# One convolution block's taps moved to TensorE, and attention values with the values stationary, in a two-layer encoder kernel

## The chip, the core and the metric

The kernel runs on one core of a Trainium2 chip. The metric is the device time of one execution in microseconds (us). A core has a matrix engine (TensorE, PE in the profile; PEld is its loading of the stationary operand), VectorE (DVE), ScalarE (ACT), GpSimd (POOL), and SyncE (SP), whose queue issues most DMAs. Each engine runs its own instructions in a fixed order. One that waits for another engine holds up everything behind it on its own engine.

## The reference

```python
for l in range(DEPTH):                       # DEPTH = 2
    x = x + 0.5 * swiglu(rms_norm(x, ffn1_norm[l]), ...)
    h = rms_norm(x, mix_norm[l]);  p = h @ w_in[l]
    attn = mla_group(...)                    # 8 heads, q and k of 96, v of 64, softmax over allowed keys
    conv = conv_group(p[..., o_cv:], ...)    # below
    x = x + jnp.concatenate([attn, conv], axis=-1) @ w_out[l]
    x = x + 0.5 * swiglu(rms_norm(x, ffn2_norm[l]), ...)
    x = rms_norm(x, post_norm[l])
...
u = a * sigmoid(g)                           # 512 channels
y = causal depthwise convolution of u, 31 taps per channel, + conv_b
conv = silu(layer_norm(y, ln_g, ln_b))
...
probs = softmax(masked scores);  out = einsum('bhqk,bhkd->bqhd', probs, v)
```

x is 512 tokens by 1024 features, float32.

## The kernel before

Activations lie with features in the 128 partitions and the 512 tokens along the row. Every large product is done as three matmuls of rounded halves (`mm3`, lines 144 to 146: hi by hi, hi by lo, lo by hi). Such a group of 24 matmuls gives 128 output features (8 blocks of 128 inputs, 3 matmuls each). `load_w` loads a weight tile over SP's queue into one of three `raw` buffers and splits it (ACT makes hi, DVE makes lo; for the output weights of kind "sum" POOL issues a DMA that adds, line 137).

A layer is FFN 1, the mixing block (`mix_body`) and FFN 2. The steps ahead of attention in the mixing block are listed in `SEQ`: c1, c2 and c3 are the input projections of the convolution's channel blocks (c0 is done ahead of the list). Each takes two groups of 24 matmuls, and then a gate (`glu`) that leaves the block's input u[c]. `uk` makes keys and values (`keys`): after its matmuls, ACT, DVE and POOL normalise the keys into `kn`, token block by token block, the last step of each being a power on POOL and products on DVE (lines 664 to 670).

Attention goes head by head in stages with lags (`ORDER`): `turn` transposes q and k of a head; `scores` makes four blocks of scores (128, 256, 384 and 512 keys wide), their maxima on DVE and the exponentials on ACT; `turn_p` transposes the exponentials in ten 128 by 128 blocks and copies them out of PSUM; `values` multiplies them with v, and for each pair of heads divides by the sums; `turn_out` transposes the pair's result, so that features are in the partitions again.

The 31 taps of the four channel blocks are applied in the ways that `CONV` names:

- "D" (c0 and c3): ACT writes the first tap and the bias into a PSUM bank (the tag "cv" has one buffer), then DVE adds 30 taps there, one instruction each (line 791), and ACT copies the bank out (line 801).
- "A" (c1 and c2): ACT makes 30 products (line 795, tag "pr", three buffers), POOL adds each of them to y (line 799). The adds of c1 from the 16th tap on and all of c2 are set to be issued after the keys' last power on POOL.

The sum of the four y (POOL, lines 813 to 815) goes into a matmul (line 817) that gives the mean for the LayerNorm. On PE the output projection's first groups (`early_groups`) stand behind that matmul. The order of instructions on each engine comes from a scheduler with its own estimate of times; it is fixed when the program is built.

Of the kernel before, what the change touches and what calls it, by code (L numbers as in the profile page):

```python
# [7 lines left out]
FP = mybir.dt.float32  # L8
# [17 lines left out]
DV = 64  # L26
# [3 lines left out]
CK = 31  # L30
# [3 lines left out]
WC = 1024  # L34
# [34 lines left out]

@with_exitstack  # L70
def encoder_kernel(ctx: ExitStack, tc: tile.TileContext, xT, consts, vecs, rgain, wgu1, wd1,
                   wcv, wql, wkl, wuq, wkv, wout, wgu2, wd2, out):
    nc = tc.nc
    PSUM = bass.MemoryType.PSUM
    cpool = ctx.enter_context(tc.tile_pool(name="const", bufs=1))
# [24 lines left out]
    V, A, G, T = nc.vector, nc.scalar, nc.gpsimd, nc.tensor  # L100
# [9 lines left out]
    ident = cst[:, CID:CID + P]  # L110
# [37 lines left out]
    def split(src, w=S):  # L148
        hi, lo = slot(FR, w), slot(FR, w)
        A.copy(hi, src)  # L150
        V.tensor_tensor(lo, src, hi.bitcast(FP), ALU.subtract)
        return hi, lo
# [350 lines left out]

    def mix_body(kpool, l, gx, norm, done):
        u, order = [], {}
        ys = [None if kind == "D" else kpool.tile([P, S], FP, tag="y", name=nm("y"), bufs=2) for kind in CONV]

        def glu(pa, pg):
            tg = tmp()
# [20 lines left out]
        cqT, ckT, pq, scqs, vs = [], [], [], [], []  # L530
# [143 lines left out]
        rm = norm()  # L674
        for step in SEQ.split():
            if step == "R":
                R = norm()
# [8 lines left out]
        at = []  # L686
# [3 lines left out]
        heads = [{} for _ in range(H)]  # L690
# [14 lines left out]
        def scores(h):  # L705
            qT, kT = heads[h]["qk"]
            b01, b2, b3 = bank(), bank(), bank()
            if h % 2 == 0:
                heads[h]["sums"] = small.tile([P, NT, 2], FP, tag="sums", name=nm("sums"), bufs=3)
            sums = heads[h - h % 2]["sums"]  # L710
            mx = small.tile([P, NT], FP, tag="mx", name=nm("mx"), bufs=3)
            pi = []
            ps = [slot() for _ in range(3)]
            ps = [ps[0][:, 0:128], ps[0][:, 128:384], ps[1][:, 0:384], ps[2]]
            for i in range(NT):
                n = (i + 1) * P
                o = (b01[:, 0:128], b01[:, 128:384], b2[:, 0:384], b3)[i]
                T.matmul(o, qT[0:DQ, i * P:(i + 1) * P], kT[0:DQ, 0:n], start=True, stop=False)  # L718
                heads[h]["s"] = T.matmul(o[:, n - 64:n], mrow, mneg, start=False, stop=True).ins
                V.tensor_reduce(mx[:, i:i + 1], o, axis=AX.X, op=ALU.max, negate=True)  # L720
# [24 lines left out]
        def values(h):  # L745

            if h % 2 == 0:
                heads[h]["po"] = bank()
            po = heads[h - h % 2]["po"].rearrange("p (t h d) -> p t h d", t=NT, h=2)
            for t in range(NT):  # L750
                for j in range(t + 1):
                    T.matmul(po[:, t, h % 2], heads[h]["pt"][j][:, (t - j) * P:(t - j + 1) * P],  # L752
                             vs[j][:, h * DV:(h + 1) * DV], start=j == 0, stop=j == t)
            if h % 2 == 0:
                return
            rs = small.tile([P, NT, 2], FP, tag="rs", name=nm("rs"))
            V.reciprocal(rs, heads[h - 1]["sums"])
            o = tmp()
            V.tensor_tensor(o.rearrange("p (t h d) -> p t h d", t=NT, h=2), po,
                            rs[:, :, :, None].to_broadcast([P, NT, 2, DV]), ALU.mult)  # L760
            heads[h]["o"] = o

        def turn_out(h):

            if h % 2 == 0:
                return
            o = heads[h]["o"]
            ps = bank()
            for t in range(NT):
                T.transpose(ps[:, t * P:(t + 1) * P], o[:, t * P:(t + 1) * P], ident)  # L770
            at.append(split(ps))

        STAGES = [({"t": turn, "s": scores, "p": turn_p, "v": values, "o": turn_out}[c], int(d)) for c, d in zip(ORDER[::2], ORDER[1::2])]
# [8 lines left out]
        cw, cb = vv(l, "cw"), vv(l, "cb")  # L782
        for c in range(4):
            kind = CONV[c]
            acc = psum.tile([P, S], FP, tag="cv", name=nm("cv"), bufs=1) if kind == "D" else ys[c]
            tap = lambda k: cw[:, c * CK + k:c * CK + k + 1]
            A.activation(acc, u[c], AF.Identity, scale=tap(CK - 1), bias=cb[:, c:c + 1])
            for k in range(CK - 2, -1, -1):
                s = CK - 1 - k
                if kind == "D":  # L790
                    V.scalar_tensor_tensor(acc[:, s:], u[c][:, :S - s], tap(k), acc[:, s:], ALU.mult, ALU.add)  # L791
                    continue
                pr = kpool.tile([P, S], FP, tag="pr", name=nm("pr"), bufs=3)
                if kind == "A":
                    A.activation(pr[:, s:], u[c][:, :S - s], AF.Copy, scale=tap(k))  # L795
                else:
                    G.tensor_scalar(pr[:, s:], u[c][:, :S - s], tap(k), None, ALU.mult)
                with tc.issue_after(order["keys"]) if s >= PAUSE or c > 1 else nullcontext():
                    order["conv"] = G.tensor_tensor(acc[:, s:], acc[:, s:], pr[:, s:], ALU.add).ins  # L799
            if kind == "D":  # L800
                A.copy(u[c], acc)
                ys[c] = u[c]
# [107 lines left out]
    for l in range(L):  # L910
# [41 lines left out]
        else:  # L952
# [3 lines left out]
            ps = spread(st3.token(D))  # L956
            for m in range(KD):
                o = slot()
# [89 lines left out]
```

## Time and profile before

| what | value |
|---|---|
| median of 3 runs (lowest to highest) | 1835.69 us (1835.47 to 1835.96) |
| profiled execution, its own time | 1836.73 us |
| span of its instructions | 1834.9 us |
| granted TensorE clock, mean of the span | 0.993 |
| PE busy, share of the span | 1793.2 us, 98% |
| DVE busy | 1347.8 us, 73% |
| ACT busy | 948.6 us, 52% |
| POOL busy | 279.0 us, 15% |

Times in the views count from the span's start. A row of the timeline has the start, the length, the engine, the line, the operation, what is written and read, the shape and the count of merged instructions; in square brackets stands the engine's idle time ahead of it and what ended that. A row of the groups by line has the count, then the busy time and the mean length of one in ns, then the idle time of the engine ahead of it. A row of the table by stage has each engine's busy time in a stretch of 20 us, and the granted clock.

### The profile page before, as it was taken

The page shows a single profiled execution, that of the slowest core. Times are in us where ns is not written, and L with a number is a line of the kernel's source. Part 1 is how long each engine was busy: PE and PEld are TensorE (multiplying, and loading weights), DVE is VectorE, ACT ScalarE, POOL GpSimd, SP SyncE. Part 2 cuts the span into 40 slices and gives each one's busy share as a digit, 9 for nine tenths or more (in the row PEclk, how much of TensorE's full clock was granted, in tenths as well). Part 3 has the DMA queues.
Part 4 walks back from the last instruction along what each step waited for, and adds up shares of the span by engine and source line. Part 5 has one row for each costly group of instructions (what it writes and reads, how often), then busy time and mean ns, then how long its engine had stood idle before and what let it go on. Part 6 is the DMA issues. An engine that isn't in the chain of part 4 may idle for free.

```text
span 1834.9 us, 22168 instructions
## 1 busy us (share of the span) xinstructions
PE 1793.2 (98%) x8512; PEld 1489.1 (81%) x8512; DVE 1347.8 (73%) x1803; ACT 948.6 (52%) x1471; POOL 279.0 (15%) x216
## 2 busy tenths in 40 slices
PE   8999999999999999999998999999999999999997
PEld 6888888888788888888877888888978788888885
DVE  8957876587957957866778667755988678577754
ACT  6534445467954634445644344444778455344442
POOL 4000000058931000000000000000688300000000
PEclk9999999999999999999999999999999999999998
DMA  8332322225134332322712332123250534323221
GB/s 294 107 123 89 117 70 69 92 87 136 25 127 106 108 123 93 105 99 69 229 66 92 107 103 92 69 71 112 76 149 1 164 89 126 115 81 115 69 70 58
DMA packets 58492, 187.95 MB, mean 102 GB/s; under 512 B 6033, under 2 KB 6417, under 8 KB 58385
## 3 DMA queue, kind: packets, MB, share of 16 engines
q1 hardware_dynamic: 54496, 173.56, 28.6%
q0 software_dynamic: 3456, 12.58, 3.9%
q8 instruction: 67, 1.10, 0.3%
q10 hardware_dynamic: 432, 0.38, 0.1%
q14 instruction: 41, 0.33, 0.1%
HBM read 184.40 MB, written 2.10 MB: 102 GB/s over the span
## 4 chain that ended last, share of the span: by engine, by line
PE 69%; issue 19%; DVE 7%; ACT 3%; POOL 2%; DMA 1%; SPq 0%; POOLq 0%; DVEq 0%; ACTq 0%
PE ps L144 21%; PE ps L146 21%; PE ps L145 20%; PE ps L752 2%; PE ps L365 1%; PE ps L718 1%; DVE wl L229 1%; ACT pr L795 1%; PE ps L739 1%; DVE fr L325 1%; DVE wl L139 1%; DVE cv L791 1%; POOL y L799 1%; POOL sck L162 0%; PE ps L182 0%
## 5 line engine op out<-in xcount | busy, mean ns | idle before, releaser
L144 PE MATMUL ps<-wh,r 128*128 128x512 f32 (+2 forms) x1392 | 525.2, 387 | 13.0 <-ACT wh L227 7.5
L145 PE MATMUL ps<-wl,r 128*128 128x512 f32 (+2 forms) x1392 | 534.5, 386 | 0.0
L146 PE MATMUL ps<-wh,r 128*128 128x512 f32 (+2 forms) x1392 | 532.1, 385 | 0.0
L227 ACT CAST wh<-fr 128x1024 fp32r<-128x1024 f32 x256 | 268.9, 1050 | 264.4 <-PE ps L146 141.3
L229 DVE TENSOR_TENSOR wl<-fr,wh 128x1024 fp32r<-128x1024 f32 x256 | 314.3, 1230 | 106.0 <-ACT wh L227 105.8
L146 PE MATMUL ps<-r,wl 128*128 128x512 f32 x1008 | 391.4, 389 | 0.5 <-POOL wl L139 0.5
L145 PE MATMUL ps<-r,wh 128*128 128x512 f32 x1008 | 391.4, 389 | 0.0
L144 PE MATMUL ps<-r,wh 128*128 128x512 f32 x1008 | 390.7, 393 | 0.3 <-ACT r L150 0.3
L144 PEld LDWEIGHTS ps<-wh,r 128*128 128x128 f32 x1392 | 262.4, 189 | 63.6 <-ACT wh L227 7.5
L145 PEld LDWEIGHTS ps<-wl,r 128*128 128x128 f32 x1392 | 262.5, 189 | 50.6 <-issue 0.5
L146 PEld LDWEIGHTS ps<-wh,r 128*128 128x128 f32 x1392 | 262.4, 188 | 50.2
L133 ACT CAST wh<-raw 128x1024 fp32r<-128x1024 f32 (+2 forms) x150 | 148.9, 997 | 217.8 <-issue 89.0
L146 PEld LDWEIGHTS ps<-r,wl 128*128 128x128 f32 x1008 | 189.2, 188 | 40.9 <-POOL wl L139 1.3
L145 PEld LDWEIGHTS ps<-r,wh 128*128 128x128 f32 x1008 | 189.2, 188 | 40.6 <-issue 1.4
L144 PEld LDWEIGHTS ps<-r,wh 128*128 128x128 f32 x1008 | 188.8, 188 | 40.9 <-ACT r L150 1.2
L139 DVE TENSOR_TENSOR wl<-raw,wh 128x1024 fp32r<-128x1024 f32 (+3 forms) x134 | 157.9, 1179 | 64.1 <-ACT wh L133 63.1
L162 POOL TENSOR_TENSOR rtok<-vtok,minus_half 128x4 f32<-128x4 f32 x9 | 11.1, 1230 | 1107.7 <-DVE vtok L188 1107.7
L443 DVE SCALAR_TENSOR_TENSOR x<-ps,x 128x512 f32<-128x512 f32 x128 | 88.2, 689 | 111.4 <-PE ps L146 110.7
L799 POOL TENSOR_TENSOR y<-y,pr 128x509 f32<-128x509 f32 (+15 forms) x120 | 157.7, 1316 | 50.2 <-ACT pr L795 42.9
L325 DVE TENSOR_TENSOR fr<-fr,fr 128x1024 f32<-128x1024 f32 x112 | 135.3, 1219 | 7.7 <-DMA fr<-in_wgu 7.2
L355 ACT ACTIVATE e<-e,rtok 128x256 f32<-128x256 f32 x120 | 61.0, 509 | 111.5 <-DVE e L346 111.2
L341 ACT COPY e<-ps 128x512 f32<-128x512 f32 x120 | 70.3, 587 | 64.1 <-PE ps L146 63.9
(165 smaller groups left out, 1731.9 us busy)
## 6 DMA issues: line engine op xcount, KB each, us to landing
fr<-in_wgu SPq DMA_DIRECT2D x176, 512.0 KB, 4.0
raw<-in_wd SPq DMA_DIRECT2D x64, 512.0 KB, 4.2
raw<-in_wd SPq DMA_DIRECT2D x32, 384.0 KB, 3.2
raw<-in_wcv SPq DMA_DIRECT2D x16, 512.0 KB, 3.3
raw<-in_wout SPq DMA_DIRECT2D x16, 512.0 KB, 3.7
raw<-in_wgu SPq DMA_DIRECT2D x8, 512.0 KB, 4.2
fr<-in_wgu POOLq DMA_DIRECT2D x8, 512.0 KB, 7.0
raw<-in_wgu POOLq DMA_DIRECT2D x8, 512.0 KB, 7.6
```

Source lines behind the costliest of these rows:

```text
L133: A.copy(hi[:, :w], raw[:, :w])
L139: (G if kind in POOLW.split() else V).tensor_tensor(lo[:, :w], raw[:, :w], hi[:, :w].bitcast(FP), ALU.subtract)
L144: T.matmul(o, lh, rh, start=first, stop=False, skip_group_check=free)
L145: T.matmul(o, lh, rl, start=False, stop=False, skip_group_check=free)
L146: T.matmul(o, ll, rh, start=False, stop=last, skip_group_check=free)
L227: A.copy(hi[:, :w], src[:, :w])
L229: V.tensor_tensor(lo[:, :w], src[:, :w], hi[:, :w].bitcast(FP), ALU.subtract)
L325: V.tensor_tensor(oh, ah, bh, ALU.add)
L341: A.copy(w[:, j, :N], o[j][:, :N])
L355: A.activation(out[j][:, :h], src[j][:, :h], AF.Silu, scale=r)
L443: V.scalar_tensor_tensor(x[:, m, :], pd, 0.5, x[:, m, :], ALU.mult, ALU.add)
L799: order["conv"] = G.tensor_tensor(acc[:, s:], acc[:, s:], pr[:, s:], ALU.add).ins
```

## The change

- The taps of block c3 go to PE (`CONV` "DAAP", function `packed`). A host-side array `wtap` holds, for each group of 32 channels and each of 8 tap groups, a 128 by 32 matrix: four tap shifts of 32 channels along its rows, diagonal in the channels. u[3] is copied by 16 DMAs (SP's queue) into four tiles, each with 32 channels four times over, shifted by 0 to 3 tokens. 32 matmuls with 32 stationary columns then add up the taps, each group of 32 channels in its own quarter of the partitions of one bank (the "cv" bank). ACT adds the bias on the way out.
- `SEQ`: c2 is projected ahead of the q latents' last step, and c3 no longer ahead of attention but between its first steps; `packed` follows at step 2.
- The exponentials are divided by their sums before they are transposed: per head one reciprocal and four DVE products from SBUF to SBUF.
- `values` has v stationary (64 columns) and the transposed probabilities moving (512, 384, 256 and 128 columns); the two heads of a pair go into the two halves of a bank's partitions. The result has features in the partitions already, so the stage `turn_out`, its transposes and the division of a pair are gone.

```diff
-CONV = "DAAD"
+CONV = "DAAP"
-SEQ = "q0 R c1 q1 q2 qo k kt tt uq uk c2 c3"
+SEQ = "q0 R c1 q1 q2 c2 qo k kt tt uq uk"
-ORDER = "t0s1p3v4o5"
+ORDER = "t0s1p3v4"
...
                 A.activation(p, o, AF.Exp, bias=mx[:, i:i + 1], ...
-                             accum_out=sums[:, i, h % 2:h % 2 + 1])
+                             accum_out=sums[:, i:i + 1])
                 pi.append(p)
+            V.reciprocal(rs, sums)
+            for i in range(NT):
+                V.tensor_scalar(pi[i], pi[i], rs[:, i:i + 1], None, ALU.mult)
...
-            po = heads[h - h % 2]["po"].rearrange("p (t h d) -> p t h d", t=NT, h=2)
-            for t in range(NT):
-                for j in range(t + 1):
-                    T.matmul(po[:, t, h % 2], heads[h]["pt"][j][:, (t - j) * P:(t - j + 1) * P],
-                             vs[j][:, h * DV:(h + 1) * DV], start=j == 0, stop=j == t)
...
-            V.reciprocal(rs, heads[h - 1]["sums"])
-            V.tensor_tensor(o..., po, rs..., ALU.mult)
-        def turn_out(h):
-            ...
-            for t in range(NT):
-                T.transpose(ps[:, t * P:(t + 1) * P], o[:, t * P:(t + 1) * P], ident)
-            at.append(split(ps))
+            po = bank()
+            for j in range(NT):
+                for e in (0, 1):
+                    T.matmul(po[e * DV:(e + 1) * DV, j * P:S], vs[j][:, (h - 1 + e) * DV:(h + e) * DV],
+                             heads[h - 1 + e]["pt"][j], start=j == 0, stop=j == NT - 1)
+            at.append(split(po))
+
+        def packed(c):
+            w = wpool.tile([P, WC], FP, tag="raw", name=nm("raw"), bufs=3)
+            nc.sync.dma_start(out=w, in_=wtap[l])
+            acc = psum.tile([P, S], FP, tag="cv", name=nm("cv"), bufs=1)
+            zs = []
+            for g in range(4):
+                t = slot()
+                V.memset(t[:, 0:4], 0.0)
+                for j in range(4):
+                    nc.sync.dma_start(out=t[32 * j:32 * j + 32, j:S], in_=u[c][32 * g:32 * g + 32, 0:S - j])
+                zs.append(t)
+            for i in range(8):
+                for g in range(4):
+                    T.matmul(acc[32 * g:32 * g + 32, 4 * i:S], w[:, (g * 8 + i) * 32:(g * 8 + i + 1) * 32],
+                             zs[g][:, 0:S - 4 * i], start=i == 0, stop=i == 7, skip_group_check=True)
+            y = slot()
+            A.activation(y, acc, AF.Identity, bias=cb[:, c:c + 1])
+            ys[c] = y
...
+                if stage is turn and step == 1:
+                    conv_in(3)
+            if step == 2:
+                packed(3)
```

In the changed file the lines move: the maxima are line 719, the exponentials 723, the new products 728, the copies of the transposed blocks 744, the values 754, the packed matmuls 772, ACT's copy of their bank 775, DVE's taps 802, ACT's products for the taps 806, POOL's adds 810, the copy of c0's bank 812, the sum 824 to 826 and its matmul 828. The scheduler sets a new order. Three places of it follow, all in the first layer (the second layer reads the same).

DVE in attention, the work of about one head, before (r_3700 is u[3], so the taps are those of c3; c0's 30 taps stand far ahead of this place, before the keys):

```order
L791 SCALAR_TENSOR_TENSOR cv_4535<-r_3700,vec,cv_4535 128x491
L742 COPY r_4026<-ps_4025 128x512
L742 COPY r_4040<-ps_4039 128x256
L791 SCALAR_TENSOR_TENSOR cv_4535<-r_3700,vec,cv_4535 128x490
L720 TENSOR_REDUCE mx_4005<-ps_4002 128x1
L791 SCALAR_TENSOR_TENSOR cv_4535<-r_3700,vec,cv_4535 128x489
L791 SCALAR_TENSOR_TENSOR cv_4535<-r_3700,vec,cv_4535 128x488
L757 RECIPROCAL rs_4226<-sums_3934 128x8
L151 TENSOR_TENSOR r_4061<-ps_4055,r_4060 128x512
L702 TENSOR_SCALAR r_4076<-ps_4071,vec 96x512
```

And after, at the same place (r_2947 is u[0]):

```order
L728 TENSOR_SCALAR r_4013<-r_4013,rs_4011 128x128
L728 TENSOR_SCALAR r_4013<-r_4013,rs_4011 128x256
L728 TENSOR_SCALAR r_4014<-r_4014,rs_4011 128x384
L728 TENSOR_SCALAR r_4015<-r_4015,rs_4011 128x512
L719 TENSOR_REDUCE mx_4088<-ps_4083 128x1
L744 COPY r_4128<-ps_4127 128x256
L702 TENSOR_SCALAR r_4144<-ps_4139,vec 96x512
L802 SCALAR_TENSOR_TENSOR cv_4349<-r_2947,vec,cv_4349 128x502
L719 TENSOR_REDUCE mx_4151<-ps_4146 128x1
L719 TENSOR_REDUCE mx_4151<-ps_4147 128x1
L719 TENSOR_REDUCE mx_4151<-ps_4148 128x1
L802 SCALAR_TENSOR_TENSOR cv_4349<-r_2947,vec,cv_4349 128x501
```

c3's taps are gone, but all 30 taps of c0 have moved from before the keys into attention, behind head 2's last maximum, since their bank is the one that `packed` holds first; four products per head are new.

DVE at the end of attention, after (r_4318 is the last pair's lo half; `cv` is c0's bank):

```order
L744 COPY r_4304<-ps_4303 128x256
L802 SCALAR_TENSOR_TENSOR cv_4349<-r_2947,vec,cv_4349 128x492
L802 SCALAR_TENSOR_TENSOR cv_4349<-r_2947,vec,cv_4349 128x491
L151 TENSOR_TENSOR r_4318<-ps_4308,r_4317 128x512
L802 SCALAR_TENSOR_TENSOR cv_4349<-r_2947,vec,cv_4349 128x490
L802 SCALAR_TENSOR_TENSOR cv_4349<-r_2947,vec,cv_4349 128x489
```

Nine taps of c0 stand behind attention's last instruction on DVE; before, c3's last tap stood ahead of the copies of the last three heads.

ACT around the packed matmuls, after (r_3149 is u[2], r_3865 is y of c3, r_3872 is q of head 3, ps_3881 to ps_3883 are scores of head 2):

```order
L806 ACTIVATE pr_4498<-r_3149,vec 128x503
L806 ACTIVATE pr_4501<-r_3149,vec 128x502
L806 ACTIVATE pr_4504<-r_3149,vec 128x501
L806 ACTIVATE pr_4507<-r_3149,vec 128x500
L775 ACTIVATE r_3865<-cv_3808,vec 128x512
L697 ACTIVATE r_3872<-ps_3867,gqs_3632 96x512
L723 ACTIVATE r_3887,sums_3884<-ps_3881,mx_3886 128x128
L723 ACTIVATE r_3888,sums_3884<-ps_3882,mx_3886 128x384
```

and before, where head 2's exponentials stand between products (ps_3807 to ps_3809 are scores of head 2):

```order
L724 ACTIVATE r_3812,sums_3810<-ps_3807,mx_3811 128x128
L795 ACTIVATE pr_4460<-r_3630,vec 128x506
L724 ACTIVATE r_3774,sums_3735<-ps_3770,mx_3773 128x256
L795 ACTIVATE pr_4463<-r_3630,vec 128x505
L724 ACTIVATE r_3813,sums_3810<-ps_3808,mx_3811 128x384
```

Before, one or two products of a tap stand between exponentials; after, 15 products stand in one piece (taps 484 to 482 of c1, then 511 to 500 of c2, by the shapes' last numbers) ahead of the copy of c3's bank, of head 3's q and of head 2's exponentials. On PE the 32 packed matmuls stand among head 0's transposes, ahead of the turns of head 4.

More of the change, by code (lines that the diff above doesn't have):

```diff
@@ L71, in encoder_kernel @@
 def encoder_kernel(ctx: ExitStack, tc: tile.TileContext, xT, consts, vecs, rgain, wgu1, wd1,
-                   wcv, wql, wkl, wuq, wkv, wout, wgu2, wd2, out):
+                   wcv, wtap, wql, wkl, wuq, wkv, wout, wgu2, wd2, out):
     nc = tc.nc
@@ L505, in mix_body @@
         u, order = [], {}
-        ys = [None if kind == "D" else kpool.tile([P, S], FP, tag="y", name=nm("y"), bufs=2) for kind in CONV]
+        ys = [None if kind in "DP" else kpool.tile([P, S], FP, tag="y", name=nm("y"), bufs=2) for kind in CONV]
         def glu(pa, pg):
@@ L707, in scores @@
             b01, b2, b3 = bank(), bank(), bank()
-            if h % 2 == 0:
-                heads[h]["sums"] = small.tile([P, NT, 2], FP, tag="sums", name=nm("sums"), bufs=3)
-            sums = heads[h - h % 2]["sums"]
+            sums = small.tile([P, NT], FP, tag="sums", name=nm("sums"), bufs=3)
+            rs = small.tile([P, NT], FP, tag="rs", name=nm("rs"), bufs=3)
             mx = small.tile([P, NT], FP, tag="mx", name=nm("mx"), bufs=3)
@@ L747, in values @@
             if h % 2 == 0:
-                heads[h]["po"] = bank()
-            po = heads[h - h % 2]["po"].rearrange("p (t h d) -> p t h d", t=NT, h=2)
-            for t in range(NT):
-                for j in range(t + 1):
-                    T.matmul(po[:, t, h % 2], heads[h]["pt"][j][:, (t - j) * P:(t - j + 1) * P],
-                             vs[j][:, h * DV:(h + 1) * DV], start=j == 0, stop=j == t)
-            if h % 2 == 0:
-                return
-            rs = small.tile([P, NT, 2], FP, tag="rs", name=nm("rs"))
@@ L757, in values @@
[L757 to L761, printed above, removed]
-        def turn_out(h):
[L765 to L768, printed above, removed]
-            for t in range(NT):
-                T.transpose(ps[:, t * P:(t + 1) * P], o[:, t * P:(t + 1) * P], ident)
-            at.append(split(ps))
@@ L773, in mix_body @@
-        STAGES = [({"t": turn, "s": scores, "p": turn_p, "v": values, "o": turn_out}[c], int(d)) for c, d in zip(ORDER[::2], ORDER[1::2])]
+                return
+            po = bank()
[22 more added lines that the diff above has]
+            ys[c] = y
@@ L774, in mix_body @@
+        cw, cb = vv(l, "cw"), vv(l, "cb")
+        STAGES = [({"t": turn, "s": scores, "p": turn_p, "v": values}[c], int(d)) for c, d in zip(ORDER[::2], ORDER[1::2])]
         for step in range(H + 6):
@@ L777, in mix_body @@
                     stage(step - lag)
+                if stage is turn and step == 1:
+                    conv_in(3)
+            if step == 2:
+                packed(3)
         with tc.issue_after(order["keys"]):
             wo = [load_w(wout[l, m], WC, "sum") for m in range(WOP)]
-        cw, cb = vv(l, "cw"), vv(l, "cb")
         for c in range(4):
             kind = CONV[c]
+            if kind == "P":
+                continue
             acc = psum.tile([P, S], FP, tag="cv", name=nm("cv"), bufs=1) if kind == "D" else ys[c]
@@ L1018 @@
     rgain = np.broadcast_to(rgain[None], (P, L, 2, DR))
+    taps = np.zeros((L, 4, 32, 4, 8, 32), f32)
+    last = a["conv_w"][:, ::-1, 3 * P:].reshape(L, CK, 4, 32)
+    for k in range(CK):
+        for c in range(32):
+            taps[:, k % 4, c, :, k // 4, c] = last[:, k, :, c]
+    taps = taps.reshape(L, P, WC)
     pos = np.arange(S, dtype=f32)
@@ L1033 @@
         "wcv": cols(np.concatenate([ca, cg], 3).reshape(L, D, 2 * CW)),
-        "wql": cols(w_in[:, :, :o1]), "wkl": rows(w_in[:, :, o1:o3]),
+        "wtap": taps, "wql": cols(w_in[:, :, :o1]), "wkl": rows(w_in[:, :, o1:o3]),
         "wuq": rows(a["w_uq"]), "wkv": rows(kv), "wout": cols(a["w_out"]),
```

## The prediction

> **What bounds the kernel now.** I read the page's first part, then the table by stage. PE is busy nearly throughout. Attention (460 to 520 us, again about 1365 to 1428) is the exception: four engines are close to full in it at once, and what counts there is which ends last.
>
> ```profile
> PE 1793.2 (98%) x8512; PEld 1489.1 (81%) x8512; DVE 1347.8 (73%) x1803; ACT 948.6 (52%) x1471; POOL 279.0 (15%) x216
> ...
> 460.00:480.00 20.00, 18.62 (x107) 12.62 (x106) 18.86 (x37) 19.97 (x50) 18.26 (x16) 0.91 0.20 36
> 480.00:500.00 20.00, 20.00 (x152) 16.75 (x152) 18.93 (x38) 19.57 (x49) 18.82 (x16) 1.00 0.00 1
> ```
>
> The timeline tells. I count from K, the end of the keys' matmuls, which is the first matmul of c2's projection (431.96 and 1340.91).
>
> ```profile
> 431.96 0.39 PE L144 MATMUL ps<-r,wh 128*128 128x512 f32 x1
> 453.72 0.60 PE L695 MATMUL ps<-cst,q 128*96 128x128 f32 x4
> 459.74 0.49 PE L718 MATMUL ps<-r,r 96*128 96x128 f32 x2 [4.11 <-ACT r L697]
> 470.84 1.29 PE L739 MATMUL ps<-cst,r 128*128 128x128 f32 x10
> 518.22 1.02 PE L817 MATMUL ps<-t,onesm 128*128 128x512 f32 x2
> 1340.91 0.39 PE L144 MATMUL ps<-r,wh 128*128 128x512 f32 x1
> 1427.19 0.59 PE L817 MATMUL ps<-t,onesm 128*128 128x512 f32 x1
> ...
> 478.04 28.78 POOL L799 TENSOR_TENSOR y<-y,pr 128x503 f32<-128x503 f32 x22 [0.38 <-ACT pr L795]
> 506.79 1.27 POOL L813 TENSOR_TENSOR t<-r,y 128x512 f32<-128x512 f32 x1
> 509.49 1.27 POOL L815 TENSOR_TENSOR t<-t,r 128x512 f32<-128x512 f32 x1
> 1386.14 28.79 POOL L799 TENSOR_TENSOR y<-y,pr 128x503 f32<-128x503 f32 x22 [0.60 <-ACT pr L795]
> ...
> 504.84 0.71 DVE L791 SCALAR_TENSOR_TENSOR cv<-r,vec,cv 128x482 f32<-128x482 f32 x1
> ```
>
> DVE's last tap ends at 505.55, POOL's sum of the four y at 510.76; the matmul that takes this sum starts at 518.22, behind attention's last transposes. So PE ends the stretch, and DVE and POOL have 12.7 and 7.5 us to spare. From K to that matmul it is 86.3 us in both layers, of which c2 and c3 are the first 21.76 (96 matmuls, 0.2267 each). The output projection stands behind that matmul on PE, so the change is worth what it does to this stretch.
>
> **The change part by part.** *c2 ahead of the keys.* 48 matmuls, 10.9 us, move to before K, where PE was full. No gain; the stretch that would leave the total as it is is now 86.3 - 10.9 = 75.4 us.
>
> *c3 among attention's first steps.* Its 10.9 us stay behind K and hide part of the keys' last work on DVE and POOL, which c2 hid too. PE will stand for some us at k's first transposes; later waits cover that, so it costs nothing of its own.
>
> *The packed taps.* fp32 goes in two passes; one row of 512 columns gives the price from start to start:
>
> ```profile
> 465.95 1.10 PE L718 MATMUL ps<-r,r 96*128 96x512 f32 x2
> 466.89 0.20 PE L719 MATMUL ps<-mneg,mrow 128*128 128x64 bf16 x1
> ...
> out_T<-r SPq DMA_DIRECT2D x8, 256.0 KB, 2.2
> ```
>
> 0.94 for 512 columns is 0.915 for the mean of 498. 32 of these are 29.3 us one after another, and 8 x 0.915 = 7.3 if the four groups run side by side. No row shows matmuls sharing the array; the nearest one speaks for 29.3, but the four read and write disjoint partitions, so I take 7.3 and keep 29.3 for the range. They stand behind head 0's first transposes, which came 17.1 us after c3 (470.84 against 453.72). c3 now ends at K + 19.4 or so (10.9, and the keys' tail), so they run from about K + 36.5 to K + 44. Their 16 copies wait on SP for DVE's memsets, some 7 us earlier; with 2.2 us to land, two rounds fit. Weights queued behind them are wanted after the stretch only.
> The Trainium skill, TensorEngine Tiling (Array Packing), section Restrictions and Gotchas, says that different row tiles can't access one PSUM bank at the same time. All four do here: by that rule it would be the 29.3.
>
> *ACT's queue: a new wait.* 15 products of taps in one piece now stand ahead of head 3's q and head 2's exponentials. They share three buffers with POOL's adds, and waiting for POOL is the only wait their line has:
>
> ```profile
> L795 ACT ACTIVATE pr<-r,vec 128x511 f32<-128x511 f32 (+14 forms) x120 | 83.4, 722 | 7.4 <-POOL y L799 7.4
> ```
>
> The last of the 15 belongs to the 27th of POOL's 45 adds behind the keys, so it waits for the 24th. The row of 22 adds above (with the sum behind it) begins with that one: it ends at 478.04 + 28.78 / 22 = 479.35, K + 47.4 (K + 46.5 in the second layer). POOL's rows ahead of it are the same, so ACT passes at K + 48, later than the packed taps. Behind it ACT has the bias copy, q, three exponentials and c0's first tap, some 5 us at 0.6 to 0.8, of which DVE can fill 2 with maxima and a copy: DVE is going again at K + 51.
>
> *DVE after that.* c3's taps are gone, but c0's 30 taps stand here now, since their bank is the one that the packed taps hold until then. 101 instructions remain up to the last: 30 taps, 20 maxima, 14 copies, 3 k scalings, 4 splits, 6 reciprocals, 24 products.
>
> ```profile
> L791 DVE SCALAR_TENSOR_TENSOR cv<-r,vec,cv 128x511 f32<-128x511 f32 (+14 forms) x120 | 87.8, 731 | 3.5 <-ACT cv L787 2.1
> L720 DVE TENSOR_REDUCE mx<-ps 128x1 f32<-128x512 f32 (+3 forms) x64 | 29.5, 480 | 5.6 <-PE ps L719 5.5
> L742 DVE COPY r<-ps 128x512 f32<-128x512 f32 (+1 forms) x32 | 16.5, 544 | 0.2 <-PE ps L739 0.2
> L702 DVE TENSOR_SCALAR r<-ps,vec 96x512 f32<-96x512 f32 x16 | 11.7, 739 | 0.1
> L151 DVE TENSOR_TENSOR r<-ps,r 128x512 fp32r<-128x512 f32 x96 | 60.5, 683 | 35.9 <-ACT r L150 35.9
> L757 DVE RECIPROCAL rs<-sums 128x8 f32<-128x8 f32 x8 | 1.5, 192 | 0.0
> ...
> 463.54 0.68 DVE L720 TENSOR_REDUCE mx<-ps 128x1 f32<-128x512 f32 x1
> 464.14 0.74 DVE L791 SCALAR_TENSOR_TENSOR cv<-r,vec,cv 128x508 f32<-128x508 f32 x1
> ```
>
> 30 x 0.731 + 20 x 0.480 + 14 x 0.544 + 3 x 0.739 + 4 x 0.683 + 6 x 0.192 = 45.2. Neighbours overlap by 0.08 (0.60 from start to start for 0.68), 77 times: 39.1. Taps that follow one another in one bank overlap less; I take 40.
>
> *The new products.* No row has one of their size. The nearest are the copies, 544 ns for the mean of 384 columns; scaled by columns the four of a head (1280 in all) cost 1.9, less overlap 1.6; six heads 9.6. From below, 24 short instructions like the reciprocal, 0.11 each, would be 2.6. I take 9.6.
> The Trainium skill, VectorE: DVE Perf Modes, section The perf-mode tier table, gives fp32 from SBUF to SBUF double rate here (2048 elements in 1227 ns); as an estimate that makes six heads about 6.5, and the total some 6 us less.
>
> *Their waits for POOL.* They touch SBUF alone, while taps, maxima and copies have a PSUM side. What happens beside POOL to the former:
>
> ```profile
> 13.09 6.41 POOL L177 TENSOR_TENSOR acc<-acc,t 128x512 f32<-128x512 f32 x4
> 15.38 2.96 DVE L255 SCALAR_TENSOR_TENSOR r<-x,vec,r 128x256 fp32r<-128x256 f32 x2
> L255 DVE SCALAR_TENSOR_TENSOR r<-x,gc,r 128x256 fp32r<-128x256 f32 x8 | 3.7, 480 | 0.0
> ...
> 415.44 2.60 POOL L799 TENSOR_TENSOR y<-y,pr 128x498 f32<-128x498 f32 x2
> 416.99 1.07 DVE L632 TENSOR_SCALAR ssh<-ssh,cq 128x8 f32<-128x8 f32 x1
> ```
>
> Two instructions of 0.48 took 2.96 while POOL added without a break: each waited for a whole add, 1.0 us more. The TENSOR_SCALAR at 416.99, of the new products' kind but with eight columns, ended with POOL's add at 418.04. From K + 48 on POOL has 21 adds left (27.5 us of the next 38), until head 5; so 16 of the 24 products, 0.7 of the time, 1.0 us: 11 us. The ends are 0 and 24 x 1.0 = 24.
>
> *The values.* 64 stationary columns and 1280 moving ones per head; turn_out's transposes and a pair's division go:
>
> ```profile
> L752 PE MATMUL ps<-r,r 128*128 128x64 f32 x320 | 39.0, 272 | 0.0
> L770 PE MATMUL ps<-cst,t 128*128 128x128 f32 x32 | 5.0, 280 | 1.6 <-DVE t L759 1.6
> ```
>
> 39.0 / 16 = 2.44 a head becomes 0.94 x 1280 / 512 = 2.35 one after another, or 1.18 if the halves run side by side. Either way PE, which waits for DVE's products, hides it, and it counts nothing; nor do the 2.5 us a layer of line 770.
>
> **The sum.** K + 51 + 40 + 9.6 + 11 = K + 111.6; then ACT's copy of c0's bank, 0.6, and POOL's three adds, 3.97 (506.79 to 510.76): the matmul at K + 116.2, against 75.4: 40.8 us later in the first layer, 39.9 in the second. PE stands over 10 us before it. The 4.11 us gap at 459.74 was followed by a granted clock of 0.91 in 20 us, a loss of 1.8; that twice, 3.6. In all 84.3 on 1836.73, 1921.0 for an execution like the profiled one; the median is 1.0 below that one, so 1920.
>
> **The rivals.** *The four groups don't run side by side.* Then c3's bank is free at K + 36.5 + 29.3 = K + 65.8 instead of the gate's K + 48, and all behind it moves by 17.8 a layer: 1956. For it: no row shows sharing. Against: disjoint partitions.
> *The products don't wait for POOL*, because ACT feeds POOL so slowly that it mostly idles. 22 us less, 1898. Against: the rows above; for it: POOL has only three buffers of products ahead of it, 3.9 us of adds, whenever ACT turns to exponentials.
> *PE stays the bound, and the time falls.* It would gain 10 us a layer in the values, 2.5 on line 770 and the 4.1 of the gap, and pay 7.3: 9.3 twice, 1817. The 98% speak for it. It needs c0's last tap by about K + 61, so all 101 instructions in the 10 us behind the gate or c0's taps elsewhere; the taps alone are 22.
>
> **How the numbers follow.** As computed 0.52, one by one 0.21, no waits 0.18, PE bound 0.04; 0.05 for an order of waits I don't see, split. The range takes the first three; its low end goes below the no-waits case, most of the way to the lower bound of the products (9.6 to 2.6 us, 14 for both layers): 1898 less 10, so 1888 to 1956. A measurement of this kernel can tell some 0.2%, 3.7 us, from no change: faster 0.04, within 0.2% 0.02, slower 0.94.
>
> **What would show it.** Right: PE idle for 10 us or more at line 828, ended by POOL's line 826, that by c0's copy on line 812; line 728 at well over 0.5 us in the mean, with POOL's adds beside it; ACT idle on line 806 behind POOL ahead of line 775. Line 772's stretch from first to last tells 7 from 29 us. I am wrong if line 828 follows line 754 without a wait, or if c0's taps end much before K + 100.

## The result and the profile after

The changed kernel takes 1898.88 us (1897.19 to 1901.02) against 1835.83 (1835.47 to 1836.46) for the kernel before, measured together: 63.05 us more, a ratio of 1.0344 with an interval of 1.0326 to 1.0362. The prediction was 1920 with a range of 1888 to 1956. The time per engine, from the page of the changed kernel:

```profile
PE 1814.5 (96%) x8416; PEld 1468.1 (77%) x8416; DVE 1343.4 (71%) x1815; ACT 954.8 (50%) x1469; POOL 277.8 (15%) x216
```

No engine has become fuller by anything like 63 us. PE is busy 21 us longer, at a mean granted clock of 0.982 for 0.993, and idle 40 us longer (span 1896.7). The timeline of the changed kernel shows where; the rows stand by engine, the first ones give K (the keys' matmuls end where q's first transposes begin) and the matmul of the mean in both layers.

```profile
442.70 0.60 PE L695 MATMUL ps<-cst,q 128*96 128x128 f32 x4
468.69 1.02 PE L772 MATMUL cv<-r,raw 128*32 128x512 f32 x2
477.28 9.15 PE L772 MATMUL cv<-r,raw 128*32 128x512 f32 x58 [1.19 <-DMA r<-r]
515.44 2.37 PE L754 MATMUL ps<-r,r 128*64 128x512 f32 x16
548.47 2.07 PE L828 MATMUL ps<-t,onesm 128*128 128x512 f32 x2 [12.79 <-POOL t L826]
1383.15 0.60 PE L695 MATMUL ps<-cst,q 128*96 128x128 f32 x4
1417.73 8.26 PE L772 MATMUL cv<-r,raw 128*32 128x512 f32 x58 [1.60 <-DMA r<-r]
1487.18 2.07 PE L828 MATMUL ps<-t,onesm 128*128 128x512 f32 x2 [12.79 <-POOL t L826]
...
440.94 6.46 POOL L162 TENSOR_TENSOR sck<-ssk,minus_half 128x8 f32<-128x8 f32 x4
485.15 0.71 ACT L806 ACTIVATE pr<-r,vec 128x500 f32<-128x500 f32 x1 [0.63 <-POOL y L810]
486.47 0.69 ACT L775 ACTIVATE r<-cv,vec 128x512 f32<-128x512 f32 x1 [0.61 <-PE cv L772]
486.84 0.42 DVE L744 COPY r<-ps 128x256 f32<-128x256 f32 x1 [12.13 <-PE ps L741]
488.90 0.75 DVE L702 TENSOR_SCALAR r<-ps,vec 96x512 f32<-96x512 f32 x1 [1.64 <-PE ps L700]
515.28 1.20 POOL L810 TENSOR_TENSOR y<-y,pr 128x482 f32<-128x482 f32 x1 [0.60 <-ACT pr L806]
536.95 6.83 DVE L802 SCALAR_TENSOR_TENSOR cv<-r,vec,cv 128x490 f32<-128x490 f32 x9
543.82 0.59 ACT L812 COPY r<-cv 128x512 f32<-128x512 f32 x1 [7.51 <-DVE cv L802]
544.48 1.26 POOL L824 TENSOR_TENSOR t<-r,y 128x512 f32<-128x512 f32 x1 [28.00 <-ACT r L812]
547.16 1.26 POOL L826 TENSOR_TENSOR t<-t,r 128x512 f32<-128x512 f32 x1
```

Read it from the end. The matmul of the mean waited 12.79 us in both layers, for POOL's sum; POOL waited 28.00 for ACT's copy of c0's bank; ACT waited for DVE's last nine taps of c0, which DVE did alone, one after another. DVE itself had stood idle for 12.13 and 1.64 us around 486.84, while ACT worked through its 15 products, twelve of them after waits of some 0.6 us for POOL, and PE through the packed taps: the first wait is for transposes that stand behind the packed taps on PE, the second for k's transposes of a later head, which stand behind PE's own wait for ACT's q. From K to the matmul of the mean it is 105.77 us in the first layer and 104.03 in the second. With 10.74 us for c2 ahead of K (442.70 against 431.96), that is 30.3 and about 28.7 more than the 86.3 of before: 59.0 of the 61.8 us by which the spans of the two profiled executions differ (1896.7 and 1834.9). In the rest there is clock, for PE, after such idle time, ran slower for a while. From the matmul of the mean to the sums of line 182, behind one group of the output projection, it is 8.90 and 8.88 us in the two layers, against 6.35 and 6.32 before: 5.1 in all. So some 2 us were won elsewhere; the record doesn't show where.

```profile
500.00:520.00 20.00, 17.34 (x95) 12.02 (x92) 20.00 (x38) 15.26 (x37) 14.88 (x12) 0.83 0.00 0
540.00:560.00 20.00, 11.53 (x42) 8.79 (x43) 8.61 (x14) 4.50 (x7) 4.82 (x4) 0.66 0.00 0
...
548.47:553.62 5.15, 5.15 (x10) 3.44 (x11) 3.04 (x5) 2.50 (x5) 0.00 (x0) 0.50 0.00 0
```

(The table by stage of the changed kernel: start and end, length, then the busy time of PE, weight loads, DVE, ACT and POOL, the granted clock, DMA.) DVE is full at 500 to 520; at 540 to 560 the granted clock is 0.66 in the mean, and 0.50 in the first 5.15 us behind the long wait.

The same table for the new products alone (line 728, DVE busy time), cut where the bank is released, where POOL's last add of a tap stands, and at c0's last tap:

```profile
486.80:515.30 28.50, 8.47 (x12) 0.88 0.06 20
515.30:543.80 28.50, 3.78 (x12) 0.87 0.00 1
```

Twelve products ahead of POOL's last add took 0.706 us each (overlaps counted once), the next twelve, of the same sizes, 0.315. By their single rows, four of the first twelve ran in a pause of POOL's adds, from 496.30 on, in 1.26 us together; the other eight took 7.2.

### The profile page after: what moved, and what is told of

Read it like the earlier page. It is cut to its first block, busy times and chain, and to the rows that moved or that the text cites. A ratio compares the mean times of both kernels' runs of the same rounds, so it can differ in the third digit from the quotient of the medians.

```text
span 1896.7 us, 22065 instructions
## 1 busy us (share of the span) xinstructions
PE 1814.5 (96%) x8416; PEld 1468.1 (77%) x8416; DVE 1343.4 (71%) x1815; ACT 954.8 (50%) x1469; POOL 277.8 (15%) x216
## 4 chain that ended last, share of the span: by engine, by line
PE 65%; issue 19%; DVE 11%; ACT 3%; POOL 2%; DMA 1%; SPq 0%; POOLq 0%; DVEq 0%; ACTq 0%
PE ps L144 20%; PE ps L146 20%; PE ps L145 20%; DVE wl L229 2%; DVE cv L802 2%; PE ps L365 1%; DVE r L728 1%; POOL y L810 1%; DVE fr L325 1%; DVE mx L719 1%; DMA fr<-in_wgu 1%; DVE r L744 1%; PE cv L772 1%; PE ps L754 1%; ACT r L723 1%
## 5 line engine op out<-in xcount | busy, mean ns | idle before, releaser
L162 POOL TENSOR_TENSOR rtok<-vtok,minus_half 128x4 f32<-128x4 f32 x9 | 13.1, 1456 | 1090.1 <-DVE vtok L188 1090.1
```

## The experiments

All times are medians of several runs against the kernel before on the same chip (1835.1 to 1835.6). The theory (A) was that of the prediction: c0's 30 taps, displaced behind the bank that the packed taps hold, end the stretch on DVE. The rivals were that the products and their waits are the cost by themselves, or that ACT's block of products holds everything.

**The parts alone.** The convolution's part:

```diff
 (changed kernel) scores, values, turn_out and ORDER as in the kernel before; CONV "DAAP", SEQ and packed as changed
```

> The convolution's part alone: packed taps and the new order of c2 and c3, but values, division and the turn of a pair as before. Theory A (c0's 30 taps, displaced behind the bank that the packed taps hold, set the end): per layer DVE is freed of 24 products behind the gate (11.8 us as they lay there in the changed kernel), takes back three divisions of a pair (some 2.5), so the mean's matmul comes about 9 us earlier in each layer than in the changed kernel: 1881 us, still 45 above before. Theory B (the products in attention and their waits are the cost, the convolution's part is harmless): within 10 us of before, 1826 to 1846.

Measured: 1876.71 us, ratio 1.0226 (1.0211 to 1.0241), 41.4 above before. The matmul of the mean comes at K + 93.3 and K + 94.7 (K is 443.46 and 1371.56), 12.5 and 9.3 us earlier than in the changed kernel, and still waits for POOL's sum:

```profile
536.75 2.08 PE L843 MATMUL ps<-t,onesm 128*128 128x512 f32 x2 [3.06 <-POOL t L841]
```

And attention's part:

```diff
 (kernel before) scores and values as changed, no turn_out; CONV "DAAD" and SEQ as before
```

> Attention's part alone: values stationary and the division ahead of the transposes; the convolution and the order of c2 and c3 as before. Theory A: DVE had 12.7 us to spare ahead of the mean's matmul; 32 products a layer are 9.4 us net alone and some 7 of waits beside POOL's adds, less four divisions of a pair (3), 13 together; so DVE and POOL end about together with where PE ended: 1836 to 1848. Theory B: most of the 63 us are here, 1870 or more.

Measured: 1862.39 us, ratio 1.0149 (1.0134 to 1.0164), 27.0 above before. Neither theory had both, and the 1862 lies between their ranges. The convolution's part costs most, and close to what A gave, but attention's part is not nearly free. In its timeline the mean's matmul waits for POOL, and POOL for DVE's last tap of c3:

```profile
515.78 1.59 PE L741 MATMUL ps<-cst,r 128*128 128x128 f32 x6 [2.55 <-DVE r L728]
530.24 2.08 PE L802 MATMUL ps<-t,onesm 128*128 128x512 f32 x2 [4.05 <-POOL t L800]
...
527.45 0.71 DVE L776 SCALAR_TENSOR_TENSOR cv<-r,vec,cv 128x482 f32<-128x482 f32 x1
```

From q's first transposes to the end of that last tap it is 73.7 us, against 51.8 before. The 32 products with their waits cover 18.0 of the 21.9; and six copies and three subtractions (4.6) that stood behind the last tap now stand ahead of it, which I hadn't counted; two divisions of a pair (1.2) are gone there. The 12.7 us that DVE had to spare were used up, and PE became the one that waits.

**c0's taps put back ahead of the keys.**

```diff
+        taps(range(1))          # c0's taps, written ahead of the stages, take the bank first
         STAGES = ...
-        for c in range(4): ...
+        taps(range(1, 4))
```

> The changed kernel, with c0's taps written ahead of attention, so that they take the bank first and go back ahead of the keys; the packed taps take the bank second. Theory A: 30 taps, 20.3 us net, leave DVE's stretch behind the gate, and the 8 us of taps alone at its end; then POOL's adds (their last at K + 74, with the sum K + 78) or PE's last values end the stretch: K + 79 instead of K + 105, 1847 us (1840 to 1856). Rival (ACT's block of products and the waits for POOL hold everything, wherever c0's taps are): 1875 to 1899.

Measured: 1864.54 us, ratio 1.0156 (1.0141 to 1.0171): 34.3 less than the changed kernel. So the displaced taps are the largest single piece, over half of the 63; the rival's 1875 is excluded. It was to be 1847 (1840 to 1856), though. POOL's sum was ready when A said (its last add ended at 522.67, K + 79.1, with K at 443.54), but the mean's matmul stood on PE behind the last heads' transposes, until 528.50:

```profile
521.40 1.27 POOL L830 TENSOR_TENSOR t<-t,r 128x512 f32<-128x512 f32 x1
528.50 1.13 PE L832 MATMUL ps<-t,onesm 128*128 128x512 f32 x2
534.14 2.37 PE L754 MATMUL ps<-r,r 128*64 128x512 f32 x14
```

**ACT's block cut up.** As e3, with the packed matmuls in four pieces (and the tap weights in a tile of their own, no longer in a `raw` buffer):

```diff
-            if step == 2:
-                packed(3)
+            if 2 <= step < 7:
+                packed(3, step - 2)     # first the copies, then 8 matmuls at each of four steps
```

> As e3, and the 32 packed matmuls are written in four pieces of 8 behind four successive heads, so that ACT's 15 products no longer stand in one piece ahead of a head's q and exponentials. Theory A: DVE's pause of 12 us ahead of the gate goes too, but POOL's 45 adds and the sum (K + 78) then end the stretch, 2 to 3 us a layer behind the 75.4 that leave the total as it was: 1841 us (1830 to 1847). Rival (the gate alone set the pace of attention, so 12 us a layer come back): 1823 or less.

Measured: 1861.52 us, ratio 1.0140 (1.0123 to 1.0157). The block was gone, and 3 us were won. The row of the products, here and in the changed kernel, tells where the rest went:

```profile
L728 DVE TENSOR_SCALAR r<-r,rs 128x128 f32<-128x128 f32 (+1 forms) x64 | 50.5, 848 | 0.4
...
484.00:504.00 20.00, 20.00 (x126) 10.55 (x118) 15.75 (x27) 14.24 (x33) 14.97 (x13) 1.00 0.00 1
...
529.92 1.13 PE L839 MATMUL ps<-t,onesm 128*128 128x512 f32 x2 [2.36 <-POOL t L837]
```

```profile
L728 DVE TENSOR_SCALAR r<-r,rs 128x128 f32<-128x128 f32 (+1 forms) x64 | 37.9, 653 | 0.1
```

0.848 us in the mean instead of 0.653. Without the block, all heads' products meet POOL's adds. The wait that was removed came back as another: POOL, which waits for ACT's products, ended its last add of a tap 6.5 us later than in e3, and its sum ended the stretch at K + 85.7.

**The packed taps in one quarter.** The changed kernel, with all four groups writing partitions 0 to 31 (and DVE clearing the bank ahead of them):

```diff
+            V.memset(acc, 0.0)
...
-                    T.matmul(acc[32 * g:32 * g + 32, 4 * i:S], ..., start=i == 0, stop=i == 7, ...)
+                    T.matmul(acc[0:32, 4 * i:S], ..., start=i == 0 and g == 0, stop=i == 7 and g == 3, ...)
```

> The changed kernel, with all 32 packed matmuls writing the same 32 partitions of the bank (the output of block c3 is then not the convolution), so that they cannot stand in different partition quarters at once. Theory A (the four groups run side by side, and DVE's work behind the bank's release sets the end): they take 32 x 0.915 = 29.3 us instead of the 8.3 to 9.2 of the changed kernel, and everything behind the release comes 20 us later in each layer: 1940 us (1930 to 1945). Rival (groups that share a bank take turns already): as the changed kernel, 1899.

```profile
476.65 26.98 PE L773 MATMUL cv<-r,raw 128*32 128x512 f32 x58 [2.34 <-DMA r<-r]
561.09 1.22 PE L829 MATMUL ps<-t,onesm 128*128 128x512 f32 x1 [12.02 <-POOL t L827]
...
L728 DVE TENSOR_SCALAR r<-r,rs 128x128 f32<-128x128 f32 (+1 forms) x64 | 27.4, 486 | 0.1
```

Measured: 1924.67 us, ratio 1.0491 (1.0473 to 1.0508): below A's range, and far from the rival's 1899. Each of these matmuls leaves two records in the trace. Their stretches, cut where the granted clock changes (length, then busy time of PE and of the weight loads, then the clock), in the changed kernel:

```profile
477.28:481.94 4.66, 4.66 (x24) 1.22 (x28) 0.50 0.00 0
481.94:486.43 4.49, 4.49 (x38) 1.09 (x30) 1.00 0.00 0
```

and in e5:

```profile
476.65:482.04 5.39, 5.39 (x7) 1.19 (x8) 0.50 0.00 0
482.04:503.62 21.58, 21.58 (x52) 5.50 (x50) 1.00 0.00 0
```

(A record that lies across a cut counts on both sides.) At a clock of 1.00 the changed kernel starts four records together every 0.42 us, e5 one every 0.41; at 0.50 both take twice as long. So it is the disjoint partitions that let the four run side by side, in one bank. The end moved by 13.1 us in the first layer (K is 442.23) and not by 20: DVE started 18 us later, but POOL's adds were then nearly over (their last ended at K + 74.9), so the products hardly waited any more (0.486 in the mean). It is e4's result from the other side.

**Without the products.** As e4, with the division on the output:

```diff
-            V.reciprocal(rs, sums)
-            for i in range(NT):
-                V.tensor_scalar(pi[i], pi[i], rs[:, i:i + 1], None, ALU.mult)
...
+            V.reciprocal(rs, heads[h - 1]["sums"])                 # of a pair
+            A.copy(rw..., rs[:, :, :, None].to_broadcast(...))     # spread over 64 columns each
+            for i in range(NT):
+                T.matmul(rb[:, i * P:(i + 1) * P], rw[:, i * P:(i + 1) * P], ident, start=True, stop=True)
+            A.copy(o, rb)
+            V.tensor_tensor(po, po, o, ALU.mult)                   # po in PSUM
             at.append(split(po))
```

> As e4, but the 32 products of a layer on DVE are gone: the sums' reciprocals of a pair are spread over the columns by ACT, turned by 4 matmuls with the identity (128 columns), copied by ACT, and DVE multiplies the pair's values in PSUM, 4 products of 0.69 a layer that have a PSUM side. Theory A (beside POOL's adds the products wait, 0.848 us in the mean in e4 against 0.37 alone, and that held attention's pace and fed POOL late): POOL's adds end near K + 75, the mean's matmul at K + 78 to 80, 3 to 5 us a layer behind before: 1840 to 1848 us. Rival (the pace of attention is not DVE's, and the products' waits were slack): 1855 or more.

Measured: 1848.58 us, ratio 1.0069 (1.0054 to 1.0084), just above what A gave; 12.9 less than e4. DVE's busy time at 484 to 504 us falls from 15.75 to 8.26 of 20, and the mean's matmul comes at K + 81.1, after a short wait for POOL's sum:

```profile
484.00:504.00 20.00, 20.00 (x143) 10.64 (x136) 8.26 (x17) 15.74 (x35) 15.91 (x13) 1.00 0.01 1
...
442.66 6.46 POOL L162 TENSOR_TENSOR sck<-ssk,minus_half 128x8 f32<-128x8 f32 x4
525.50 1.13 PE L847 MATMUL ps<-t,onesm 128*128 128x512 f32 x2 [0.47 <-POOL t L845]
```

So 50 of the 63 us are accounted for by removing three things in turn: 34.3 by c0's place, 3.0 by the block, 12.9 by the products. (The last is net of the work of the new division.) POOL's sum lets the mean's matmul start 5.7 and 3.8 us behind the K + 75.4 that would leave the total as it was, at K + 81.1 and K + 79.2; that is most of the 13 us that remain. But PE was done only 0.47 us sooner, so an earlier sum alone would win little.

**Fewer adds behind the keys,** in e6:

```diff
-PAUSE = 16
+PAUSE = 24
```

> As e6, and POOL adds c1's first 23 products ahead of the keys instead of the first 15 (PAUSE 24 for 16). Theory A (POOL's sum ends the stretch in e6): eight adds less behind the keys, 10.4 us, the mean's matmul at K + 68 to 71: 1822 to 1830 us, faster than before. Rival (something else ends it): as e6 within 5 us; a second one: the eight adds delay the keys' own steps on POOL, and nothing is won.

Measured: 1871.99 us, ratio 1.0201 (1.0184 to 1.0218). The second rival had the direction: POOL's four powers for the keys start 6 us later than in e6, and K with them (450.32 for 444.42). The loss of 23 us is more than these 6 in each layer: in the second, K is 12.0 us behind e6's (1372.23 for 1360.21) and the mean's matmul 18.2 (1457.56 for 1439.41). What holds attention up behind K stays open. The row of e7, to be held against that of e6 above:

```profile
448.79 6.43 POOL L162 TENSOR_TENSOR sck<-ssk,minus_half 128x8 f32<-128x8 f32 x4
```

**The kernel before with the new values and the division on the output:**

```diff
 (e2) with the division of e6
```

> The kernel before (convolution and its order untouched) with the values stationary and the division on the output as in e6, so without the 32 products. Theory A (in e2 the 32 products, 18 us net a layer with their waits, made DVE's last tap the end): DVE ends some 16 us earlier than in e2, PE has 10 us a layer less in the values and 2.5 less in the turn of a pair, and pays 16 matmuls of 128 columns, 3.5: 1820 us (1813 to 1832), faster than before. Rival (the new form of the values itself costs, by waits on PSUM or in ACT): 1840 or more.

Measured: 1834.87 us, ratio 0.9998 (0.9989 to 1.0008): no difference, and between A's range and the rival's. Without the products e2's whole loss (27.0 us) is gone. But PE saves some 8 us a layer (10 in the values and 2.5 in the turn of a pair, less 4 times 1.16 for the turned reciprocals), and that doesn't show in the time. The mean's matmul comes 3.4 us earlier in the first layer (514.81 for 518.22), but 2.37 us of the last pair's values, which stood ahead of it before, now stand behind it. Two stages:

```profile
454.00:474.00 20.00, 15.93 (x88) 11.01 (x87) 17.24 (x32) 19.97 (x45) 19.01 (x17) 0.91 0.45 98
474.00:494.00 20.00, 18.12 (x118) 12.53 (x119) 19.11 (x36) 19.99 (x50) 18.23 (x15) 1.00 0.00 1
```

PE now has idle time there, and ACT has none: 19.97 and 19.99 of 20, as in the kernel before (19.97 and 20.00). I read ACT as what sets the pace, but it isn't shown: e11, below, takes four copies a layer off ACT and is no faster.

**Two attempts at more.** e9 is e6, and e10 is e8, with copies moved from ACT to DVE and the mean made by two matmuls, the second with c2's y; e11 and e12 have the copies alone. (`EVP` names the engines that copy the transposed blocks in turn: D is DVE, A is ACT.)

```diff
-            A.copy(o, rb)                                   # e9 to e12
+            V.tensor_copy(o, rb)
-EVP = "DAD"                                                 # e9, e12
+EVP = "DDD"
-        (G if YP else V).tensor_tensor(ysum, ysum, ys[3], ALU.add)    # e9, e10: ysum of ys[0], ys[1], ys[3]
-        T.matmul(pm, onesm, ysum, start=True, stop=True)
+        T.matmul(pm, onesm, ysum, start=True, stop=False)
+        T.matmul(pm, onesm, ys[2], start=False, stop=True)
-            A.activation(tiny("pre", 1), ysum[:, 0:1], AF.Silu)
+            A.activation(tiny("pre", 1), ys[2][:, 0:1], AF.Silu)
```

> As e6, with three things moved: all copies of transposed blocks on DVE (which is 8 to 11.8 us busy of 20 in e6's attention) instead of a third on ACT, the copy of the turned reciprocals on DVE, and the mean from two matmuls (the sum of y of c0, c1 and c3 early, then y of c2), so that POOL has no add behind its last tap. Theory A (e6 ends with POOL's adds, which ACT feeds late, and two adds behind them, 2.6 us): the mean's matmuls come 4 to 9 us a layer earlier than in e6: 1830 to 1841 us, about as before or a little faster. Rival (PE is the bound in e6, 20.0 of 20 at 484 to 504 us): within 4 us of e6, 1845 to 1852.

> As e8, with the copy of the turned reciprocals on DVE and the mean from two matmuls as in e9 (the other copies as before, since DVE still has c3's taps here). Theory A (ACT, 19.97 and 19.99 of 20 us busy at 454 to 494, and POOL's last two adds hold e8): 2 to 4 us a layer, 1827 to 1831 us. Rival (PE's own tail holds it): within 2 us of e8.

> Half of e10: the copy of the turned reciprocals on DVE, the mean from one matmul as in e8. If the second matmul of the mean cost e10 its 9 us, this one is at 1829 to 1835 us, at or a little below before; if the moved copies (and the new order of ACT and PE with them) cost it, 1842 to 1846.

> e9 without the mean's second matmul: all copies of transposed blocks and of the turned reciprocals on DVE. If the second matmul of the mean (it stood behind groups that wait for the last pair's values) cost e9 its 25 us, this one is at 1836 to 1846 us, below e6; if the moved copies cost it, 1860 to 1875.

Measured: e9 1873.37 (1.0209, 1.0195 to 1.0223) and e10 1844.12 (1.0049, 1.0036 to 1.0063), both slower and outside every range given; e11 1834.92 (0.9994, 0.9985 to 1.0003) and e12 1846.69 (1.0058, 1.0044 to 1.0072). The moved copies change nearly nothing. The edit for the mean cost 27 and 9 us. Part of that was my own slip: the small Silu that loads ACT's table ahead of time read c2's y, which ACT writes early, so it ran early. By the groups of e9 there are four loads ahead of line 512 in the two layers, where e6 has two, and two more ahead of line 865, where e6 has none:

```profile
L512 ACT ACT_TABLE_LOAD x4 | 5.1, 1283 | 0.1
L865 ACT ACT_TABLE_LOAD x2 | 2.6, 1283 | 20.4 <-DVE t L863 20.4
```

Four loads more, at 1.28 us, are 5 us and not 27. More lies in the second matmul's place: on PE it stands behind the last pair's values, and in the first layer of e9 the mean is complete at 532.83 instead of 526.63 in e6, though its first matmul starts at 525.35, as early as e6's. (In e10 the second matmul stands ahead of these values, at 518.51.) In e9 PE is 10.9 us behind e6 where it goes on with the output projection (550.41 for 539.50). How this divides between the place, the loads and the clock was not separated. No version beat the kernel before by more than a measurement can tell.

## Why the prediction came out as it did

The mechanism was right in the order it was told: the taps of c0 behind the gate (the point where ACT is past its 15 products and c3's bank is done), DVE's chain up to K + 101.1, ACT's copy, POOL's sum, a long wait at line 828 ended by line 826. The point was 21 us too high, 10.4 and 11.3 in the two layers. That the result is the number of the rival without waits (1898) is chance: the waits were there, smaller, and other terms were off as well. For the first layer, term by term:

- *The gate, K + 48.* ACT's last product ended at K + 43.2, and ACT took the packed taps' bank at K + 43.8 (486.47), 0.6 later, when PE was done with it; in the second layer ACT was the later one, as forecast. I had taken POOL's rows of before as they were; but with c2 out of the way the keys' last power ended on POOL at 447.40, K + 4.7. In the kernel before it ended at 443.22, K + 11.3. Off by 4.2.
- *DVE going again at K + 51.* K + 46.2 (488.90): 2.4 behind the gate for the 3 that I gave. Off by 0.6.
- *The new products, 9.6.* Twelve of them without POOL took 3.78, so 24 are 7.6 alone. The copies were the wrong neighbour: 128 to 512 columns took 0.27, 0.34, 0.41 and 0.47 us, hardly a copy's 0.54 for 384. The Trainium skill, VectorE: DVE Perf Modes, section The perf-mode tier table, was nearer with 6.5, and the trace agrees with its double rate: the products grow by 0.53 ns a column (0.27 us at 128, 0.47 at 512), DVE's copies out of PSUM by 1.07 (0.41 us at 256, 0.68 at 512). Off by 2.0.
- *Their waits, 11.* This is the term that was mis-sized most: 4.7 (twelve at 0.706 less twelve at 0.315). I charged 16 products a whole add each. Only eight met adds, since POOL's last add of a tap ended at 516.48, K + 73.8, sooner than I had it, and one head's four fell into a pause ahead of that; and of a head's four two waited for a whole add and one for a part, not all: the median of the first layer's 32 is 0.410, the longest 1.486. Off by 6.3.

```profile
L728 DVE TENSOR_SCALAR r<-r,rs x32: 268/410/1486, 467.1 to 528.4; 128x128 f32<-128x128 f32 x8, 128x256 f32<-128x256 f32 x8, 128x384 f32<-128x384 f32 x8, 128x512 f32<-128x512 f32 x8
```

- *DVE's other work, 40.* 54.9 us from 488.90 to 543.78 less 12.25 for products leaves 42.6, 2.2 of it idle. Off by 2.6 the other way.
- *Copy and sum, 4.6:* 4.7. *Clock, 3.6 in all:* 5.1, by the two stretches above.

The sum, 4.2 + 0.6 + 2.0 + 6.3 - 2.6 - 0.1, is the 10.4.

*The packed taps* ended where I put them for a wrong reason. They began 10 us earlier than forecast (468.69, K + 26) and then waited for the copies of u[3]: 2.29, 1.16 and 1.19 us, which I had said would fit; SP issued the 16 one after another in 10.99 us. The 7.3 was about right at a clock of 1.00, where 64 records at four in 0.42 us are 6.7. That the last 58 took 9.15 and 8.26 us is the clock of 0.50 in the first 4.66 and 2.87 of them, after these waits. That the groups run side by side was right. The rule that I set against it (the Trainium skill, TensorEngine Tiling (Array Packing), section Restrictions and Gotchas) speaks of row tiles. These matmuls each read all 128 rows (not disjoint ones, as I wrote) and use 32 columns, so they are column tiles: I applied a sentence to a case it doesn't cover, and gave its rival 0.21 in part for that. e5 shows that its price was too high too, 26 us and not 36, since products that come later don't wait.

*The values* were right: 2.37 us a pair, so 1.18 a head, with the halves side by side, and they counted nothing.

## What to carry to other kernels

Where two steps share one buffer, the order in which the code first takes it is an instruction to the scheduler: here it moved 30 instructions of an unrelated block to the worst place, for 34 of 63 us. Before charging an operation with another engine's waits, find out until when that engine has work at all, and how many of a group really start second; and expect such waits to grow when something else is sped up (0.486, 0.653 and 0.848 us for the same products in e5, the changed kernel and e4). An engine that is given time where several are near full doesn't give it back by itself: e8 saved PE some 8 us a layer and won nothing, with ACT at 19.99 of 20 beside it.

## What the runs showed of the hardware

- Four float32 matmuls of 32 columns into the four quarters of one bank run fully side by side: four records every 0.42 us at a granted clock of 1.00, against one every 0.41 us in one quarter. A mean over the whole stretch (0.158 against 0.465) hides this, since the clock was 0.50 in a different share of each.
- A product on DVE from SBUF to SBUF, 0.27 to 0.47 us alone, took up to 1.49 us while POOL added without a break; taps, maxima and copies with a PSUM side beside them kept their 0.73, 0.48 and 0.54. The Trainium skill, SBUF — State Buffer, section SBUF: two separate sides, says that whichever of the two starts first holds a shared pair of ports for the whole instruction. The rows agree, and POOL waits too: its add at 496.74, when a head's products had started first, took 1.93 us, and its adds grew from 1.316 to 1.343 us in the mean.
